# Attention with probabilities times values in plain float32, two groups of four heads in one PSUM tile

## The chip, the core and the metric

The kernel runs on one core of a Trainium2 chip. The metric is the device time of one execution in microseconds (us), as the median of several runs. The profile comes from one further execution, recorded instruction by instruction.

## The reference

A decoder trunk with two layers: sliding-window attention, then gated DeltaNet. 2048 tokens of width 1024 follow 16 meta tokens. Only the attention layer matters here (16 heads of 64, two heads of keys and values, so 8 query heads to each):

```python
s_band = einsum('bnqhgd,bnkhd->bnhgqk', qb, k_band) * scale      # blocks of 128 queries, 256 keys
s_meta = einsum('bnqhgd,bmhd->bnhgqm', qb, k_meta) * scale       # 16 meta tokens
s_band = where(valid_band, s_band - slopes * clipdist(dist_band), -inf)
s_meta = where(valid_meta, s_meta - slopes * clipdist(dist_meta), -inf)
p = softmax(concatenate([s_band, s_meta, sink], -1))
o = einsum(p_band, v_band) + einsum(p_meta, v_meta)
return (o * silu(gate)) @ w_out
```

Everything is float32 for the reference.

## The kernel before

The program is unrolled and built from tiles. A planner orders the instructions of each engine ahead of time from priorities (`high_priority(offset=...)` raises those of a block) and puts in all semaphores; at run time each engine takes its own list in order. A tile pool has a fixed number of buffers for each tag, and a new tile waits until the oldest is released.

Products that need float32 accuracy are mostly made in a reduced format (`F32R`, called fp32r in the profile): an operand is split into a high part, the cast, and a low part, the rest, and two or three products are added in PSUM. `mm3` (L60 to L63) makes three, `split` (L55 to L57) the two parts. A product of two plain `F32` tiles needs no split.

The stages: `attn_proj` (input projection; q, k, v and the gate go to DRAM; the gate comes last, transposed, with its store in L232), `attention`, then the DeltaNet stages `dn_proj` and `dn_scan`, which the change does not touch apart from comments. `attn_consts` runs between the q, k, v columns and the gate and makes masks and what belongs to the meta tokens.

`attention` goes over 17 tiles of tokens: 16 meta tokens, then 16 blocks of 128. A tile has four calls of `scores` and four of `values`, each for a group `hg` of 4 heads; `values` of a group comes four groups behind its `scores` (LAG, L493).

- `prep` (L335 to L377) loads q, k and v of the next tile and transposes them on TensorE; v is split into high and low halves of `vt` (L359, L360). The gate tile (L374) has one buffer.
- `scores` (L379 to L418), for each head: two products of the queries with 272 keys into `s_ps` (two buffers), then one VectorE operation that adds the distances and keeps the maximum (L395). For the 4 heads together: `nb`, `es` (L399 to L402), four exponentials on ScalarE (L405), the sum and its reciprocal (L408, L409). The meta probabilities are scaled (L411) and split into `px` on GpSimd (L413, L414); the band's are scaled on GpSimd (L416).
- `values` (L420 to L463), for 4 heads: the meta probabilities are transposed (L426) and copied into `mt` in four copies of 32 partitions, two on VectorE, two on ScalarE (L431, L433), so that each head's rows stand in its own columns only. Each of the two blocks of 128 keys is transposed, 4 heads into one PSUM tile (L440, pools `pt0` and `pt1`, one buffer each), then split: ScalarE casts `ph`, VectorE subtracts into `pl` (L443, L444). Five products of 512 columns go into `pv` (L447 to L449; one buffer): the stationary operand is 64 high and 64 low columns of v, so the upper 64 partitions of `pv` hold the part that comes from low v. ScalarE copies that part to `ob` (L451), VectorE adds it in two operations, one for each parity of heads, into `ot` (L453). GpSimd multiplies by the gate (L461), ScalarE and GpSimd split into `oh` and `ol` (L462, L463).
- `finish` (L465 to L478) is the output projection of a tile, 48 products of 512 columns by `mm3` into `ps_o`, cut into pieces that go between the other work.

Of the kernel before, what the change touches and what calls it, by code (L numbers as in the profile page):

```python
# [15 lines left out]
P = 128  # L16
# [22 lines left out]
def rsqrt(nc, pool, y, x, shape, tag):  # L39
    """y = x ** -0.5 for positive normal x."""  # L40
# [37 lines left out]
def norm_rows(nc, small, scr, xt, n, eng=None):  # L78
    """xt[:n] = rms_norm(xt[:n]) without its weight, which goes into the rows of the projection"""
# [15 lines left out]
def transpose_split(nc, psum, ident, xt, n, hi, lo, c0):  # L95
    """hi/lo[:, kt, c0:c0+n] = split(xt[:n].T)"""
# [10 lines left out]
def attn_proj(tc, a, sc, ident, hook):  # L107
    """q (normalised, ALiBi-scaled), k (normalised, twice), v and silu(gate)^T to DRAM."""
# [4 lines left out]
    with (  # L113
# [48 lines left out]
        def qkv_tile(cols, m, r0):  # L162
            """cols: (number of the column block, its weights)"""
# [52 lines left out]
        for c0 in (5, 7):  # L216
# [7 lines left out]
            for e, ct, (t0, n, hi, lo) in order:  # L224
# [7 lines left out]
                nc.sync.dma_start(sc["gate"][(c0 - 5 + e) * 2 + ct, :, t0:t0 + n], st[:, :n])  # L232


def attn_consts(tc, a, sc, ident, kp, tpp):
    """Masks with the distances, sinks, and what the meta tokens are as keys and values."""
# [43 lines left out]
    # v of the meta tokens, 8 times: for the high and the low parts of the probabilities of 4 heads  # L280
    vm = kp.tile([P, P], F32, name="vm")
    vmeta = kp.tile([P, 2, P], F32R, name="vmeta")
    for j in range(8):
        nc.sync.dma_start(vm[j * 16:j * 16 + 16, :], sc["kv"][0:NMETA, 256:384])
    vs = vm.rearrange("p (k d) -> p k d", k=2)
    split(nc, vmeta[:, :, 0:64], vmeta[:, :, 64:128], vs)
    return dict(tabs=tabs, sink=sink, sinkp=sinkp, nslope=nslope, wkk=wkk, kmeta=kmeta, vmeta=vmeta)


def attention(tc, a, sc, ident, ac):  # L290
    nc = tc.nc
    v = nc.vector
    with (
        tc.tile_pool(name="p2q", reuse_waits="tile", bufs=2) as lq,
        tc.tile_pool(name="p2s", reuse_waits="tile", bufs=4) as sp,
        tc.tile_pool(name="p2k", reuse_waits="tile", bufs=2) as lk,
        tc.tile_pool(name="p2p", reuse_waits="tile", bufs=5) as lx,
# [7 lines left out]
        tc.tile_pool(name="p2pt", reuse_waits="tile", bufs=2, space=PSUM) as tpp,  # L305
# [6 lines left out]
        tabs, sink, sinkp, nslope, wkk, kmeta, vmeta = (  # L312
# [985 lines left out]
```

## Time and profile before

| | |
|---|---|
| median of 3 runs | 3212.55 us (3207.07 to 3213.83) |
| span of the profiled execution | 3218.0 us |
| TensorE matmuls busy | 2994.2 us, 93% |
| VectorE busy | 2240.6 us, 70% |
| ScalarE busy | 1488.4 us, 46% |
| GpSimd busy | 969.5 us, 30% |
| TensorE clock granted, mean | 0.975 |

In the profile PE is TensorE's matmuls, PEld its weight loads, DVE VectorE, ACT ScalarE, POOL GpSimd, SP the engine that issues most DMAs. A row names the source line, the engine, the operation, the tile written and the tiles read. Matmuls overlap with one another, and a row's length has the way through the array in it, so the step from start to start tells what a product takes away from the next one, and its length doesn't. Shares of busy time are means over stages with different limits, so the stage of the change is read by itself.

### The profile page before, as it was taken

What the parts mean: (1) busy time and instruction counts of PE and PEld (TensorE: products, weight loads), DVE (VectorE), ACT (ScalarE), POOL (GpSimd) and SP (SyncE); (2) the same over time, 40 slices, a digit from 0 to 9 for tenths busy, and PEclk for the clock granted to TensorE, in tenths of its full rate; (3) what the DMA queues carried; (4) which work ended last, traced back from release to release, by engine and by line L of the source; (5) the groups of instructions that cost most, each with busy time, mean ns of one, the idle gap of its engine ahead of it and who ended that gap; (6) DMA issues with size and microseconds to landing.
All of it is one profiled execution on the core that took longest, in us unless ns stands there. A gap on an engine that the chain in (4) does not pass through costs nothing.

```text
span 3218.0 us, 54338 instructions
## 1 busy us (share of the span) xinstructions
PE 2994.2 (93%) x18685; PEld 2643.1 (82%) x18685; DVE 2240.6 (70%) x6092; ACT 1488.4 (46%) x4247; POOL 969.5 (30%) x1118
## 2 busy tenths in 40 slices
PE   6999998988888999999999989899989999999899
PEld 6999996776666999888999989898976777777687
DVE  6786028999897767897825767988148777788632
ACT  5513147776665453443325344332245665566421
POOL 3011004555453332321112222222144444444100
PEclk9999999999999999999999999999998999999899
DMA  4323122222223345346442434456455666565442
GB/s 116 98 70 100 60 81 91 80 77 67 71 75 101 102 114 128 101 123 167 145 115 78 121 102 111 104 145 192 129 158 146 171 184 182 170 173 159 153 139 98
DMA packets 553595, 385.92 MB, mean 120 GB/s; under 512 B 245512, under 2 KB 505352, under 8 KB 546152
## 3 DMA queue, kind: packets, MB, share of 16 engines
q1 hardware_dynamic: 517032, 365.05, 40.0%
q10 hardware_dynamic: 35952, 16.80, 1.9%
q0 software_dynamic: 336, 0.60, 0.3%
q8 instruction: 148, 2.42, 0.3%
q14 instruction: 127, 1.04, 0.1%
HBM read 245.38 MB, written 136.97 MB: 119 GB/s over the span
## 4 chain that ended last, share of the span: by engine, by line
PE 53%; DVE 27%; DMA 7%; ACT 6%; issue 5%; POOL 2%; SPq 1%; DVEq 0%; ACTq 0%; POOLq 0%
PE ps_d L61 5%; PE ps_d L62 5%; PE ps_d L63 5%; PE ps_o L61 4%; PE ps_o L62 4%; PE ps_o L63 4%; DVE acc L768 4%; PE r_ps L1110 3%; PE ds_ps L1137 3%; PE ps_mm L63 2%; PE ps_mm L61 2%; PE ps_mm L62 2%; DVE Xt L910 2%; PE o_ps L1141 2%; PE vn_ps L1126 2%
## 5 line engine op out<-in xcount | busy, mean ns | idle before, releaser
L61 PE MATMUL ps_d<-y_hi,wi_hi 128*128 128x384 f32 (+2 forms) x2304 | 752.4, 327 | 45.0 <-ACT u L762 38.5
L63 PE MATMUL ps_d<-y_hi,wi_lo 128*128 128x384 f32 (+2 forms) x2304 | 744.8, 323 | 0.0
L62 PE MATMUL ps_d<-y_lo,wi_hi 128*128 128x384 f32 (+2 forms) x2304 | 744.3, 323 | 0.0
L61 PEld LDWEIGHTS ps_d<-y_hi,wi_hi 128*128 128x128 f32 x2304 | 441.3, 192 | 59.0 <-ACT u L762 44.1
L63 PEld LDWEIGHTS ps_d<-y_hi,wi_lo 128*128 128x128 f32 x2304 | 441.8, 192 | 3.7 <-issue 3.4
L62 PEld LDWEIGHTS ps_d<-y_lo,wi_hi 128*128 128x128 f32 x2304 | 441.9, 192 | 1.9 <-issue 1.8
L640 POOL TENSOR_TENSOR wi_raw<-wi_raw,nw 128x1024 f32<-128x1024 f32 x96 | 207.2, 2159 | 642.0 <-DMA wi_raw<-in_dn_w_in 603.2
L57 DVE TENSOR_TENSOR wi_lo<-wi_raw,wi_hi 128x1024 fp32r<-128x1024 f32 x96 | 125.9, 1311 | 273.7 <-ACT wi_hi L56 270.8
L768 DVE SCALAR_TENSOR_TENSOR acc<-u,cw,acc 128x1040 f32<-128x1040 f32 (+1 forms) x192 | 284.4, 1481 | 6.4
L1112 POOL TENSOR_TENSOR S<-S,eL 128x256 f32<-128x256 f32 x248 | 157.6, 644 | 197.0 <-PE r_ps L1110 130.9
L61 PE MATMUL ps_o<-wo,oh 128*128 128x512 f32 x512 | 209.4, 409 | 3.7 <-ACT oh L56 2.9
L63 PE MATMUL ps_o<-wo,ol 128*128 128x512 f32 x512 | 204.7, 400 | 0.0
L1119 ACT ACTIVATE qs<-r_ps,ea 64x128 f32<-64x128 f32 x512 | 182.4, 362 | 47.1 <-DVE xp L1117 37.3
L62 PE MATMUL ps_o<-wo,oh 128*128 128x512 f32 x512 | 203.4, 397 | 0.0
L63 PE MATMUL ps_mm<-w_hi,y_lo 128*128 128x256 f32 (+1 forms) x680 | 193.2, 287 | 5.1 <-DVE y_lo L104 5.1
L61 PE MATMUL ps_mm<-w_hi,y_hi 128*128 128x256 f32 (+1 forms) x680 | 193.6, 287 | 4.0 <-DVE st L190 3.1
L1117 DVE SCALAR_TENSOR_TENSOR xp<-r_ps,c,bv_t 64x128 f32<-64x128 f32 x512 | 174.6, 343 | 30.3 <-ACT qs L1119 11.4
L62 PE MATMUL ps_mm<-w_lo,y_hi 128*128 128x256 f32 (+1 forms) x680 | 193.4, 286 | 0.0
L56 ACT CAST wi_hi<-wi_raw 128x1024 fp32r<-128x1024 f32 x96 | 100.5, 1046 | 160.2 <-PE ps_d L62 133.4
L1110 PE MATMUL r_ps<-S,kq_t 128*128 128x256 f32 x512 | 163.4, 407 | 4.3 <-ACT qs L1119 3.8
L405 ACT ACTIVATE p<-p,nb 128x272 f32<-128x272 f32 (+2 forms) x272 | 134.0, 495 | 51.2 <-DVE nb L400 50.7
L762 ACT COPY u<-ps_d 128x384 f32<-128x384 f32 (+2 forms) x192 | 84.1, 439 | 157.9 <-PE ps_d L63 157.8
(311 smaller groups left out, 7168.2 us busy)
## 6 DMA issues: line engine op xcount, KB each, us to landing
wi_raw<-in_dn_w_in SPq DMA_DIRECT2D x96, 512.0 KB, 4.3
kq_t<-d_kq SPq DMA_DIRECT2D x33, 512.0 KB, 5.8
bv_t<-d_bv SPq DMA_DIRECT2D x33, 512.0 KB, 5.2
x_t<-in_x SPq DMA_DIRECT2D x32, 512.0 KB, 3.6
d_kq<-kq SPq DMA_DIRECT2D x16, 1024.0 KB, 5.2
d_bv<-bv SPq DMA_DIRECT2D x32, 512.0 KB, 5.2
kt_t<-d_ktok SPq DMA_DIRECT2D x64, 256.0 KB, 4.3
z_t<-d_z SPq DMA_DIRECT2D x16, 1024.0 KB, 6.8
```

Of the source, the lines that this page charges most:

```text
L56: nc.scalar.copy(hi, src)
L57: nc.vector.tensor_tensor(lo, src, hi.bitcast(F32), op=ALU.subtract)
L61: nc.tensor.matmul(ps, lhsT=lh, rhs=rh, start=start, stop=False)
L62: nc.tensor.matmul(ps, lhsT=lh, rhs=rl, start=False, stop=False)
L63: nc.tensor.matmul(ps, lhsT=ll, rhs=rh, start=False, stop=stop)
L405: nc.scalar.activation(p4[:n, hh, k0:272], p4[:n, hh, k0:272], AF.Exp, bias=nb[:n, hh:hh + 1], scale=SLOPES[hg * 4 + hh], accum_out=z[:n, ...
L640: nc.gpsimd.tensor_tensor(raw, raw, nw.unsqueeze(2).to_broadcast([P, KT, P]), op=ALU.mult)
L768: v.scalar_tensor_tensor(acc[:, :ncol], in0=u[:, j:j + ncol], scalar=cw[:, ct, j:j + 1], in1=acc[:, :ncol], op0=ALU.mult, op1=ALU.add)
L1110: nc.tensor.matmul(r, lhsT=kq[:, g, :], rhs=S[:, g], start=True, stop=True)
L1112: nc.gpsimd.tensor_tensor(S[:, g], S[:, g], pers["eL"][hf][:, :, g, n].unsqueeze(2).to_broadcast([P, 2, P]), op=ALU.mult)
L1117: v.scalar_tensor_tensor(xp[hb[h]], in0=r[0:64, h, :], scalar=pers["c1"][hf][hb[h], g, n:n + 1], in1=bv[hb[h], g, :], op0=ALU.mult, op1=AL ...
L1119: nc.scalar.activation(qs[hb[h]], r[64:128, h, :], AF.Copy, scale=pers["ea"][hf][hb[h], g, n:n + 1])
```

## The change

Eight heads, all that share one head of keys and values, are handled in one call, and the calls become generators that the outer loop takes forward in five steps for each group, with pieces of `prep` and `finish` between them.

- The product of probabilities and values is made in plain float32: v goes in straight from the loaded tile `kv` as 64 stationary columns, the transposed probabilities as plain float32 `ph` (copied, three of four times by ScalarE, once by VectorE). `pl`, `vt`, `px`, `ob` and the additions into `ot` are gone.
- Heads 0 to 3 of a group (e = 0) go to partitions 0 to 63 of `pv`, heads 4 to 7 (e = 1) to 64 to 127.
- The meta probabilities are transposed unsplit, 8 heads by 16 rows; one VectorE operation makes `mt` by a product with a mask `mrow`.
- VectorE multiplies `pv` by the gate as it reads it. The order of heads in `ot` differs, so the gate is stored in another order (two DMAs in place of one) and the rows of the output weights are loaded in another order (two DMAs in place of one).
- The gate tile has two buffers, `kv` four, `ph` six; the two pools of transposed probabilities become one with two buffers; `p8` has three buffers of 8 heads where `p4` had five of 4.

Comments that the diff takes away elsewhere are left out here.

```diff
...
-                nc.sync.dma_start(sc["gate"][(c0 - 5 + e) * 2 + ct, :, t0:t0 + n], st[:, :n])
+                for x in range(2):
+                    hd = ((c0 - 5 + e) * 2 + ct) * 2 + x
+                    r = hd % 8 // 4 * 64
+                    nc.sync.dma_start(sc["gate"][hd // 8 * 4 + hd % 4, r:r + 64, t0:t0 + n],
+                                      st[x * 64:x * 64 + 64, :n])
...
-    vm = kp.tile([P, P], F32, name="vm")
-    vmeta = kp.tile([P, 2, P], F32R, name="vmeta")
+
+    vmeta = kp.tile([P, 2, 2, 64], F32, name="vmeta")
+    nc.gpsimd.memset(vmeta, 0.0)
     for j in range(8):
-        nc.sync.dma_start(vm[j * 16:j * 16 + 16, :], sc["kv"][0:NMETA, 256:384])
-    vs = vm.rearrange("p (k d) -> p k d", k=2)
-    split(nc, vmeta[:, :, 0:64], vmeta[:, :, 64:128], vs)
-    return dict(tabs=tabs, sink=sink, sinkp=sinkp, nslope=nslope, wkk=wkk, kmeta=kmeta, vmeta=vmeta)
+        nc.sync.dma_start(vmeta[j * 16:j * 16 + 16, j // 4],
+                          sc["kv"][0:NMETA, 256:384].rearrange("m (k d) -> m k d", k=2))
+
+    mrow = kp.tile([P, 4], F32, name="mrow")
...
+    return dict(tabs=tabs, sink=sink, sinkp=sinkp, nslope=nslope, wkk=wkk, kmeta=kmeta, vmeta=vmeta, mrow=mrow)
...
-        tc.tile_pool(name="p2s", reuse_waits="tile", bufs=4) as sp,
+        tc.tile_pool(name="p2s", reuse_waits="tile", bufs=3) as sp,
         tc.tile_pool(name="p2k", reuse_waits="tile", bufs=2) as lk,
-        tc.tile_pool(name="p2p", reuse_waits="tile", bufs=5) as lx,
+        tc.tile_pool(name="p2p", reuse_waits="tile", bufs=3) as lx,
...
-        tc.tile_pool(name="p2p0", reuse_waits="tile", bufs=1, space=PSUM) as pt0,
-        tc.tile_pool(name="p2p1", reuse_waits="tile", bufs=1, space=PSUM) as pt1,
+        tc.tile_pool(name="p2p0", reuse_waits="tile", bufs=2, space=PSUM) as ptp,
...
+            w = a["attn_w_out"][0].rearrange("(v e h d) c -> v h e d c", v=2, e=2, h=4)
             for k in range(KT):
                 for c in range(2):
                     raw = lk.tile([P, 512], F32, tag="wraw", name="wo_raw")
                     cs = slice(c * 512, c * 512 + 512)
-                    nc.sync.dma_start(raw, a["attn_w_out"][0][k * P:(k + 1) * P, cs])
+                    for e in range(2):
+                        nc.sync.dma_start(raw[e * 64:e * 64 + 64], w[k // 4, k % 4, e, :, cs])
                     split(nc, who[k][:, cs], wlo[k][:, cs], raw)
...
-                kv = lq.tile([P, 384], F32, tag="kv", name="kv_t")
+                kv = lq.tile([P, 384], F32, tag="kv", bufs=4, name="kv_t")
...
-                vt = wk.tile([P, 2, P], F32R, tag="vt", name="vt")
-                vsrc = kv[:, 256:384].rearrange("p (k d) -> p k d", k=2)
-                nc.scalar.copy(vt[:, :, 0:64], vsrc)
-                nc.gpsimd.tensor_tensor(vt[:, :, 64:128], vsrc, vt[:, :, 0:64].bitcast(F32), op=ALU.subtract)
...
-            gt = lp.tile([P, KT, P], F32, tag="gate", bufs=1, name="gate_t")
+            gt = lp.tile([P, KT, P], F32, tag="gate", bufs=2, name="gate_t")
...
+        def scores(t, kvh):
...
+                if hh in (1, 3, 5):
+                    yield
...
-            pm = lx.tile([P, 4, 16], F32, tag="pm", bufs=5, name="pm")
-            v.tensor_tensor(pm[:n], p4[:n, :, 256:272], z[:n].unsqueeze(2).to_broadcast([n, 4, 16]), op=ALU.mult)
-            px = lx.tile([P, 4, 2, 16], F32R, tag="px", bufs=5, name="px")
-            nc.gpsimd.tensor_copy(px[:n, :, 0], pm[:n])
-            nc.gpsimd.tensor_tensor(px[:n, :, 1], pm[:n], px[:n, :, 0].bitcast(F32), op=ALU.subtract)
+            pm = lx.tile([P, 8, 16], F32, tag="pm", name="pm")
+            v.tensor_tensor(pm[:n], p8[:n, :, 256:272], z[:n].unsqueeze(2).to_broadcast([n, 8, 16]), op=ALU.mult)
             if i is not None:
-                nc.gpsimd.tensor_tensor(p4[:n, :, k0:256], p4[:n, :, k0:256],
-                                        z[:n].unsqueeze(2).to_broadcast([n, 4, 256 - k0]), op=ALU.mult)
-            c["p", hg] = (p4, px)
-
-        def values(t, hg):
-            """Attention output of 4 heads, transposed."""
+                for e in range(2):
+                    es_ = slice(e * 4, e * 4 + 4)
+                    nc.gpsimd.tensor_tensor(p8[:n, es_, k0:256], p8[:n, es_, k0:256],
+                                            z[:n, es_].unsqueeze(2).to_broadcast([n, 4, 256 - k0]), op=ALU.mult)
+            c["p", kvh] = (p8, pm)
+            yield
...
+
             c = ctx[t]
-            n, i, kvh, ot = c["n"], c["i"], hg // 2, wk.tile([P, 2, P], F32, tag="ot", name="ot")
-            p4, px = c.pop(("p", hg))
+            n, i = c["n"], c["i"]
+            p8, pm = c.pop(("p", kvh))
+            blocks = [] if i is None else [(128, c["kv"])] if i == 0 else [(0, ctx[t - 1]["kv"]), (128, c["kv"])]
             tm = tpp.tile([P, P], F32, tag="tp", bufs=2, name="tm")
-            nc.tensor.transpose(tm[:, :n], px[:n].rearrange("p h e m -> p (h e m)").bitcast(F32), ident[:n, :n])
...
+            nc.tensor.transpose(tm[:, :n], pm[:n].rearrange("p h m -> p (h m)"), ident[:n, :n])
+            mt = wk.tile([P, 4, P], F32, tag="mt", bufs=2, name="mt")
+            v.tensor_tensor(mt[:, :, :n], tm[:, :n].unsqueeze(1).to_broadcast([P, 4, n]),
+                            mrow.unsqueeze(2).to_broadcast([P, 4, n]), op=ALU.mult)
+            terms = []
+            for b0, kv in blocks:
+                for e in range(2):
+                    pt = ptp.tile([P, 4, P], F32, tag="pt", name="pt")
+                    for hh in range(4):
+                        nc.tensor.transpose(pt[:, hh, :n], p8[:n, e * 4 + hh, b0:b0 + 128], ident[:n, :n])
+                    ph = wk.tile([P, 4, P], F32, tag="ph", bufs=6, name="ph")
+                    if e and b0:
+                        v.tensor_copy(ph[:, :, :n], pt[:, :, :n])
+                    else:
+                        nc.scalar.copy(ph[:, :, :n], pt[:, :, :n])
+                    terms.append((e, kv[:, 256 + kvh * 64:256 + kvh * 64 + 64], ph))
+                    yield
+            terms += [(e, vmeta[:, e, kvh, :], mt) for e in range(2)]
             pv = vpp.tile([P, 4, P], F32, tag="pv", name="pv")
...
+            for j, (e, vt, ph) in enumerate(terms):
+                nc.tensor.matmul(pv[e * 64:e * 64 + 64, :, :n], lhsT=vt, rhs=ph[:, :, :n], start=j < 2,
+                                 stop=j >= len(terms) - 2)
+            if kvh == 0:
                 c["xt"] = xp.tile([P, D], F32, tag="x", name="x_t")
                 nc.sync.dma_start(c["xt"][:n], x_rows(a, i))
                 c["oh"] = lp.tile([P, KT, P], F32R, tag="oh", name="oh")
                 c["ol"] = lp.tile([P, KT, P], F32R, tag="ol", name="ol")
-            ks = slice(hg * 2, hg * 2 + 2)
+            ks = slice(kvh * 4, kvh * 4 + 4)
             oh, ol = c["oh"][:, ks, :n], c["ol"][:, ks, :n]
-            nc.gpsimd.tensor_tensor(ot[:, :, :n], ot[:, :, :n], c["gt"][:, ks, :n], op=ALU.mult)
+            ot = wk.tile([P, 4, P], F32, tag="ot", bufs=2, name="ot")
+            v.tensor_tensor(ot[:, :, :n], pv[:, :, :n], c["gt"][:, ks, :n], op=ALU.mult)
             nc.scalar.copy(oh, ot[:, :, :n])
             nc.gpsimd.tensor_tensor(ol, ot[:, :, :n], oh.bitcast(F32), op=ALU.subtract)
+            yield
 
...
-        slots = [(t, hg) for t in range(len(tiles)) for hg in range(4)]
+        slots = [(t, kvh) for t in range(len(tiles)) for kvh in range(2)]
 
         fin = None
         pre = None
-        LAG = 4
+        LAG = 2
         for j in range(len(slots) + LAG):
-            with tc.high_priority(offset=150 + (1000 if j < 12 else 0)):
-                if j < len(slots):
-                    t, hg = slots[j]
-                    if hg == 0:
+            boost = 1000 if j < 6 else 0
+            sg = vg = None
+            if j < len(slots):
+                t, kvh = slots[j]
+                with tc.high_priority(offset=150 + boost):
+                    if kvh == 0:
                         for _ in pre or ():
                             pass
                         pre = prep(t + 1) if t + 1 < len(tiles) else None
-                    scores(t, hg)
-                    next(pre, None) if pre else None
-                    next(pre, None) if pre and hg == 0 else None
-            with tc.high_priority(offset=250 + (1000 if j < 12 else 0)):
-                if j >= LAG:
-                    t, hg = slots[j - LAG]
-                    if hg == 3:
-                        for _ in fin or ():
-                            pass
-                    values(t, hg)
-                    if hg == 3:
-                        fin = finish(t)
-            for _ in range(2):
-                next(fin, None) if fin else None
+                sg = scores(t, kvh)
+            if j >= LAG:
+                t, kvh = slots[j - LAG]
+                if kvh == 1:
+                    for _ in fin or ():
+                        pass
+                vg = values(t, kvh)
+            for step in range(5):
+                with tc.high_priority(offset=150 + boost):
+                    next(sg, None) if sg else None
+                    if step in (1, 2, 4) and pre:
+                        next(pre, None)
+                with tc.high_priority(offset=250 + boost):
+                    next(vg, None) if vg else None
+                if step < 4 or not vg:
+                    next(fin, None) if fin else None
+            if j >= LAG and slots[j - LAG][1] == 1:
+                fin = finish(slots[j - LAG][0])
...
```

## Rows read from the trace of the kernel before

**Rows 1.** Page, part 2: busy tenths of two engines in 40 slices

```profile
PE   6999998988888999999999989899989999999899
...
DVE  6786028999897767897825767988148777788632
```

**Rows 2.** Stretches: length, then each engine's busy us and instructions, clock, DMA

```profile
300.00:475.00 175.00, 174.32 (x982) 166.63 (x981) 25.12 (x104) 50.37 (x123) 13.95 (x24) 1.00 0.25 80
475.00:1010.00 535.00, 467.53 (x2427) 368.46 (x2425) 473.01 (x1480) 369.15 (x1120) 267.49 (x376) 0.97 0.25 80
...
560.00:990.00 430.00, 378.02 (x1981) 301.46 (x1980) 383.16 (x1160) 291.37 (x886) 222.76 (x307) 0.98 0.23 74
```

**Rows 3.** Who TensorE's products waited for, 560 to 990 us: total, times, longest

```profile
PE pv L447 <- DVE ot L453: 18.1, 21, 3.0
PE pt L440 <- DVE pl L444: 10.8, 20, 1.5
PE s_ps L393 <- DVE mx L395: 9.0, 19, 1.0
PE tm L426 <- DVE mt L431: 6.4, 5, 2.2
```

**Rows 4.** VectorE by line, 475 to 1010 us: busy us, mean ns, idle

```profile
L444 DVE TENSOR_TENSOR pl<-pt,ph 128x512 fp32r<-128x512 f32 x124 | 84.3, 684 | 10.1 <-ACT ph L443 9.2
L453 DVE TENSOR_TENSOR ot<-pv,ob 64x256 f32<-64x256 f32 x128 | 53.0, 414 | 3.8 <-ACT ob L451 2.2
...
L431 DVE CAST mt<-tm 32x128 fp32r<-32x128 f32 x128 | 37.1, 290 | 6.7 <-ACT mt L433 2.7
L399 DVE TENSOR_TENSOR nb<-mx,sinkp 128x4 f32<-128x4 f32 x64 | 24.6, 384 | 0.9
...
L400 DVE TENSOR_TENSOR nb<-nb,nslope 128x4 f32<-128x4 f32 x64 | 21.4, 334 | 1.0
```

**Rows 5.** ScalarE by line, same stretch

```profile
L443 ACT CAST ph<-pt 128x512 fp32r<-128x512 f32 x124 | 70.7, 584 | 26.4 <-PE pv L447 25.3
...
L451 ACT COPY ob<-pv 64x512 f32<-64x512 f32 x64 | 37.3, 583 | 3.3 <-PE pv L449 1.9
...
L433 ACT CAST mt<-tm 32x128 fp32r<-32x128 f32 x128 | 32.5, 254 | 41.9 <-DVE mt L431 32.2 <-PE tm L426 8.0
```

**Rows 6.** GpSimd by line, same stretch

```profile
L461 POOL TENSOR_TENSOR ot<-ot,gate_t 128x256 f32<-128x256 f32 x64 | 47.4, 741 | 88.3 <-DVE ot L453 85.3 <-DMA gate_t<-d_gate 3.0
...
L414 POOL TENSOR_TENSOR px<-pm,px 128x64 fp32r<-128x64 f32 x64 | 20.6, 322 | 2.2
L413 POOL CAST px<-pm 128x64 fp32r<-128x64 f32 x64 | 16.0, 250 | 11.5 <-DVE pm L411 4.6 <-PE pv L449 2.3 <-DVE nb L399 2.3
```

**Rows 7.** Timeline: start and length in us, engine, line, operation, idle before

```profile
704.33 0.84 DVE L453 TENSOR_TENSOR ot<-pv,ob 64x256 f32<-64x256 f32 x2
...
705.33 0.47 PE L447 MATMUL pv<-ph,vt 128*128 128x512 f32 x1 [0.59 <-DVE ot L453]
...
705.63 0.39 PE L448 MATMUL pv<-pl,vt 128*128 128x512 f32 x1
...
706.32 0.39 PE L449 MATMUL pv<-mt,vmeta 128*128 128x512 f32 x1
```

**Rows 8.** Timeline of TensorE in the scan of the DeltaNet stage

```profile
2599.80 0.38 PE L1110 MATMUL r_ps<-S,kq_t 128*128 128x256 f32 x1
...
2601.08 0.61 PE L1110 MATMUL r_ps<-S,kq_t 128*128 128x256 f32 x2
```

**Rows 9.** Timeline of TensorE in the DeltaNet projection

```profile
1201.77 1.04 PE L813 MATMUL tp_k<-ident,kq 128*128 128x128 f32 x8
1202.74 1.09 PE L848 MATMUL g_ps<-kq 128*64 128x128 f32 x16
1203.76 0.45 PE L61 MATMUL ps_d<-y_hi,wi_hi 128*128 128x400 f32 x1
```

**Rows 10.** The products into g_ps: ns shortest, median, longest; first and last start

```profile
L848 PE MATMUL g_ps<-kq x528: 272/273/444, 1087.7 to 2179.7; 128*64 128x128 f32 x176
```

More of the change, by code (lines that the diff above doesn't have):

```diff
@@ L304, in attention @@
         tc.tile_pool(name="p2x", reuse_waits="tile", bufs=2) as xp,
[L305 removed]
+        tc.tile_pool(name="p2pt", reuse_waits="tile", bufs=1, space=PSUM) as tpp,
         tc.tile_pool(name="p2ps", reuse_waits="tile", bufs=2, space=PSUM) as spp,
         tc.tile_pool(name="p2pv", reuse_waits="tile", bufs=1, space=PSUM) as vpp,
[L308 to L309 removed]
+        tc.tile_pool(name="p2p0", reuse_waits="tile", bufs=2, space=PSUM) as ptp,
         tc.tile_pool(name="p2pp", reuse_waits="tile", bufs=1, space=PSUM) as pp,
     ):
[L312 to L317 removed]
+        tabs, sink, sinkp, nslope, wkk, kmeta, vmeta, mrow = (
+            ac[n] for n in ("tabs", "sink", "sinkp", "nslope", "wkk", "kmeta", "vmeta", "mrow"))
         who, wlo = [], []
@@ L343, in prep @@
             if i is None:
-                kwin = vt = None
+                kwin = None
             else:
@@ L427, in values @@
-            mt = mts[hg % 2]
-            for hh in range(4):
-                ps = slice(hh * 32, hh * 32 + 32)
-                if hh % 2:
-                    v.tensor_copy(mt[ps, hh, :n], tm[ps, :n])
-                else:
-                    nc.scalar.copy(mt[ps, hh, :n], tm[ps, :n])
-            blocks = [] if i is None else [(128, c["vt"])] if i == 0 else [(0, ctx[t - 1]["vt"]), (128, c["vt"])]
-            pv = vpp.tile([P, 4, P], F32, tag="pv", name="pv")
-            pts = []
-            for (b0, vt), ptp in zip(blocks, (pt0, pt1)):
-                pt = ptp.tile([P, 4, P], F32, tag="pt", name="pt")
-                for hh in range(4):
-                    nc.tensor.transpose(pt[:, hh, :n], p4[:n, hh, b0:b0 + 128], ident[:n, :n])
-                ph = wk.tile([P, 4, P], F32R, tag="ph", name="ph")
-                pl = wk.tile([P, 4, P], F32R, tag="pl", name="pl")
-                nc.scalar.copy(ph[:, :, :n], pt[:, :, :n])
-                v.tensor_tensor(pl[:, :, :n], pt[:, :, :n], ph[:, :, :n].bitcast(F32), op=ALU.subtract)
-                pts.append((vt, ph, pl))
@@ L446, in values @@
-            for bi, (vt, ph, pl) in enumerate(pts):
-                nc.tensor.matmul(pv[:, :, :n], lhsT=vt[:, kvh, :], rhs=ph[:, :, :n], start=bi == 0, stop=False)
-                nc.tensor.matmul(pv[:, :, :n], lhsT=vt[:, kvh, :], rhs=pl[:, :, :n], start=False, stop=False)
-            nc.tensor.matmul(pv[:, :, :n], lhsT=vmeta[:, kvh, :], rhs=mt[:, :, :n], start=not blocks, stop=True)
-            ob = wk.tile([64, 4, P], F32, tag="ob", bufs=2, name="ob")
-            nc.scalar.copy(ob[:, :, :n], pv[64:128, :, :n])
@@ L478, in finish @@
             yield
-        def run(gen, k=1):
-            for _ in range(k):
-                if gen is None or next(gen, 0) == 0:
-                    return
         with tc.high_priority(offset=200):
```

49 lines of the change are left out of this document (27 added, 22 removed).

## The prediction, made before the changed kernel ran

> **What bounds the kernel now.** I read the shares of the span in slices first, to find the stage that the change touches. The attention is the stretch of 80 us slices in which VectorE stands at 8 or 9 tenths and TensorE at 8 to 9 [rows 1]; before it VectorE is nearly idle and TensorE full. Then the table by stretches: from 475 to 1010 us, the 535 us in which attention runs, TensorE is busy 467.5 us, VectorE 473.0, ScalarE 369.2, GpSimd 267.5 [rows 2]. No engine is full. TensorE idles 535 - 467.5 = 67.5 us, and of these 430 - 378.0 = 52.0 lie in the even middle from 560 to 990 us. In the projection ahead, from 300 to 475 us, TensorE is busy 174.3 of 175 us [rows 2]. So these 67.5 us are what this stage could give back at most, as long as TensorE's own work doesn't grow.
>
> Third, who makes TensorE wait in that middle. All the long waits are on VectorE: 18.1 us of pv for the additions into ot, 10.8 of the transposes for pl, 9.0 of the scores for the maximum, 6.4 of the transposed meta probabilities for the copies into mt [rows 3]. The timeline shows one such wait: the two additions run from 704.33 to 705.17, TensorE stands 0.59 us, then the five products of 512 columns follow, the second at 705.63 and the fifth at 706.32, so 0.23 us apart [rows 7]. So VectorE, at 88 to 89% and in order, holds up an in-order TensorE. The question is whether the change takes more from that chain than it puts on TensorE.
>
> **The change part by part, for 8 heads (two calls of values before, one after); 32 of them, two with one block of keys in place of two, and two small ones for the 16 meta tokens, which I leave out.**
>
> VectorE loses pl (124 x 0.684 = 84 us), the two additions into ot (128 x 0.414 = 53), half of the mt copies (128 x 0.290 = 37) [rows 4]. It gains, for each 8 heads, three operations on 128 x 512 from PSUM: the product that makes mt, the product with the gate and one copy ph. I price them as pl, which reads the same shape from PSUM, at 0.684: 3 x 0.684 x 32 = 66. The copy has no row of its own; its bounds are ScalarE's 0.584 for the same shape [rows 5] and pl's 0.684, no matter here. The small operations on 4 columns become half as many on 8; the two steps of nb alone are 24.6 + 21.4 us, so half of them is -23 [rows 4]. VectorE: 473 - 84 - 53 - 37 + 66 - 23 = 342 us of 535.
>
> ScalarE loses ob (37.3), its half of mt (32.5) and a quarter of the ph copies (70.7 / 4 = 18) [rows 5]: 369 - 88 = 281. GpSimd loses the gate (47.4) and the split of px (20.6 + 16.0) [rows 6]: 267 - 84 = 183. None of the three can bound the stage any more. TensorE is the only engine left near it.
>
> TensorE. Before, 8 heads take 10 products of 512 columns at 0.23 us from start to start [rows 7]: 2.30 us. After, they take 6 products in plain float32. How long is one? The state product r_ps is plain float32 of 256 columns. It stands as two records, 0.61 us together where one alone is 0.38, so the second starts 0.23 us behind the first [rows 8]; that is twice the time for a column of the reduced format, and twice over. For 512 columns that makes 2 x 2 x 0.23 = 0.92 us. g_ps gives it finer and shows something else: eight plain float32 products of 64 stationary columns, which go by turns to the lower and the upper 64 partitions of one tile, are 16 records of 128 columns in 1.09 us; the 8 transposes ahead of them, of 128 columns too and one behind the other, take 1.04 [rows 9]. So two records go side by side: less the 0.27 us of the last one [rows 10], seven steps take 0.82 us, 0.12 each with a longer first one, and the transposes' 0.77 / 7 = 0.11. I take 0.11 us for each pair. The new pv products are made the same way (64 stationary columns, e = 0 to the lower, e = 1 to the upper partitions, in turns). At 512 columns a pair of records is 4 x 0.11 = 0.44 us, a pair of products 0.88, three pairs 2.64: +0.34 us on the 2.30. One transpose of px less is -0.11. Going into and out of the half-width form costs 0.2 us in place of 0.11, read from the last transpose to the first g_ps and from the last g_ps to ps_d [rows 9]: +0.2 for both. Sum +0.43 us for 8 heads, 32 times: +14 us.
>
> The trace has no pair in which the second product has to wait for a copy of its own. In the change each ph comes from its own copy, and between the products the planner may put transposes or scores, which break a pair. Per 8 heads the cost of this lies between 0 and three lone products, 3 x 0.88 = 2.64 us. I take one lone product more in every fourth group, 0.88 x 8 = +7 us, near the lower end: the five old pv products stand back to back in the timeline, though four of them hang on copies of their own [rows 7].
>
> The idle time. The waits for ot, pl and the mt copies are 18.1 + 10.8 + 6.4 = 35.3 of the 52 us [rows 3]. The operations behind them go: pv is now released by one operation in place of the copy ob and two additions, half as often; pt is released by one copy in place of copy and subtraction; mt by one operation in place of eight copies. In proportion, over the whole stage, 35.3 x 67.5 / 52 = 46 us. I let the wait for the maximum and the rest stand, since the 16 maxima of a tile stay as they are. What is late next is TensorE itself.
>
> A new wait: the gate product waits on VectorE for the last pv product, and behind it queue the maxima of the next heads, for which the scores wait with two buffers. Before, the additions into ot stood in the same place. So I add nothing, with 0.68 us x 32 = 22 us as the upper bound and zero below.
>
> Hidden edits: the gate's store is two DMAs in place of one (five column chunks by eight blocks, 40 to 80), on SP's queue in the stretch in which TensorE is full [rows 2]; kv_t, q_t and the output weights queue behind them, so without that cover it would be a late start of attention, at most some us. The loads of the output weights double in number and keep their bytes. The zeroing of vmeta, mrow and its transpose come once, in the same stretch. The second gate buffer can only help. I keep 5 us each way for the start and the end of the stage.
>
> Sum: -46 + 14 + 7 = -25 us. The profiled execution spans 3218.0 us, 0.2% over the median of 3212.55; the stage's difference is taken off the median: 3187.5, so 3187 us.
>
> One rule of the Trainium skill speaks against the change. FP8 and Floating Point Precision, TensorE Precision Notes, says that true FP32 takes four passes through the array; the trace agrees for one product alone, 0.92 us against 0.23. By that rule without the side-by-side halves, the sum is that of the first rival.
>
> **The rivals.**
> First, the pairs don't form, and it gets slower. Mechanism: a product of e = 0 is queued as soon as its ph is there, transposes or scores stand between it and its partner, and each runs alone. All six alone are 5.28 us in place of 2.64, +2.64 x 32 = +84, and with -46 + 14 the kernel comes to +52: 3265. Two lone products more in each group would give -32 + 56 = +24: 3236. It decides from 32 / 32 = 1 us, a little over one lone product for 8 heads. For it: old pv had to wait for its buffer, which let its copies pile up; new pv doesn't have to. Against it: g_ps, and e alternates, so that a shifted pair is still a pair.
> Second, the waits move: with two groups in flight in place of four, a chain of 8 maxima, 8 exponentials and two products on GpSimd has less slack, and TensorE waits for the probabilities or for ScalarE's copies. If 21 of the 46 us stay lost, the sum is near zero: 3212. For it: the chain of 8 heads is twice as long and one buffer less is free. Against it: ScalarE and GpSimd fall to about 281 and 183 of 535 us.
> Third, TensorE closes nearly all gaps: -67 + 14 = -53: 3159.
>
> **How the numbers follow.** Forecast 0.58, first rival 0.20, second 0.12, third 0.10. The likeliest one's own range is 3170 to 3205 (the bounds of the new wait and of the ends). The range for 8 in 10 takes in most of the third and the milder half of the first rival: 3157 to 3238. A difference of 0.2%, 6.4 us, is about what can be told from none. Faster is the forecast's 0.57 and the third's 0.10, a little of the others: 0.68. Same is most of the second: 0.12. Slower is the first: 0.20.
>
> **What would show it.** In the changed profile: the stage's VectorE near 340 us, ScalarE near 280, GpSimd near 185; pv records of 128 x 512 with 64 columns that start within some ns of each other, two by two, and a fresh pair each 0.44 us; no wait of TensorE for an operation behind pv that costs over a few us in total. Wrong it is if pv records start alone, one each 0.43 us with other products between them; if TensorE's idle time in the stage stays near 67 us under new names (ph, p, z); or if the stage's gain is there and the DeltaNet stages behind it, which no line of the change touches, give it back.

## The result, and the profile of the changed kernel

The changed kernel takes **3230.31 us** as the median of 20 runs (3213.39 to 3240.85), the kernel before 3213.19 us (3200.37 to 3221.29, 20 runs beside it): ratio **1.0055, interval [1.0042, 1.0067]**. It is 17 us slower, where 25 us faster had been forecast. The profiled execution of the changed kernel spans 3214.7 us, at the low end of its runs. The two profiled executions differ by 9 us ahead of the change already (the last product of the q, k, v columns starts at 300.0 us before, at 291.0 after), and by another 9 us behind it, in the DeltaNet stages that no line of the change touches (2212.7 us before, 2203.9 after). So the stage is compared by itself and not by the spans.

First the stretches of the changed kernel, columns as in [rows 2]: length, busy us and instructions of TensorE, its weight loads, VectorE, ScalarE and GpSimd, clock, DMA.

```profile
475.00:1010.00 535.00, 515.01 (x2395) 326.05 (x2394) 316.31 (x967) 258.84 (x787) 170.94 (x129) 0.97 0.25 78
560.00:990.00 430.00, 420.15 (x1972) 267.54 (x1973) 250.74 (x742) 200.94 (x617) 143.96 (x101) 0.99 0.23 70
```

In these 535 us VectorE falls from 473.0 to 316.3 us, ScalarE from 369.2 to 258.8, GpSimd from 267.5 to 170.9. TensorE's idle time falls from 67.5 to 20.0 us, and in the even middle from 52.0 to 9.9 us. All this is what the change was to do. But the stage has become longer. From the last product of the gate to the last product of attention's output it takes 517.3 us before (488.0 to 1005.3) and 532.4 after (478.4 to 1010.8): +15.1 us, near the 17 us between the medians.

Who TensorE waited for in the changed kernel, 560 to 990 us (total, times, longest), against [rows 3]:

```profile
PE tm L441 <- DVE pm L425: 5.0, 5, 1.3
PE s_ps L405 <- DVE mx L407: 4.2, 14, 0.5
PE ps_o L61 <- DVE x_t L487: 0.3, 1, 0.3
PE qps L377 <- DVE mt L443: 0.2, 1, 0.2
```

The waits for ot, pl and mt (35.3 us) are gone, and no wait for ph, p or z has taken their place. TensorE is now itself what is late. In the chain of waits over the whole span its share goes from 53% to 64%, VectorE's from 27% to 21%; these lines begin part 4 of the page, before and after:

```profile
PE 53%; DVE 27%; DMA 7%; ACT 6%; issue 5%; POOL 2%; SPq 1%; DVEq 0%; ACTq 0%; POOLq 0%
```

```profile
PE 64%; DVE 21%; DMA 5%; ACT 4%; issue 3%; POOL 1%; SPq 1%; DVEq 0%; ACTq 0%; POOLq 0%
```

What TensorE does with the time is seen in the table of stretches for the products into pv alone (length, busy us and records, clock, DMA): before, then after.

```profile
475.00:1010.00 535.00, 96.69 (x314) 0.97 0.25 80
```

```profile
475.00:1010.00 535.00, 153.09 (x380) 0.97 0.25 78
```

The pv products take 56 us more. The records give the balance of the whole stage, when the time from each start to the next is put down to the product that started first (idle time falls to the product ahead of it):

| from the last gate product to the last output product, us | before | after | |
|---|---|---|---|
| pv | 88.4 | 147.5 | +59.1 |
| scores | 121.2 | 104.2 | -17.0 |
| transposes | 93.5 | 77.6 | -15.9 |
| output projection | 214.2 | 203.2 | -11.0 |
| stage | 517.3 | 532.4 | +15.1 |

So three kinds of work give back 44 us, and pv takes 59. The timeline of TensorE in the changed kernel shows how (start and length in us, line, operation, tile, shape, count):

```profile
705.39 0.39 PE L63 MATMUL ps_o<-wo_hi,ol 128*128 128x512 f32 x1
705.71 1.07 PE L461 MATMUL pv<-ph,kv_t 128*64 128x512 f32 x2
706.72 0.66 PE L450 MATMUL pt<-ident,p 128*128 128x128 f32 x4
707.13 0.37 PE L405 MATMUL s_ps<-kwin,qst 128*128 128x272 f32 x1
707.34 0.29 PE L406 MATMUL s_ps<-kwin,qst 128*128 128x272 f32 x1
707.46 0.27 PE L450 MATMUL pt<-ident,p 128*128 128x128 f32 x1
707.66 1.07 PE L461 MATMUL pv<-ph,kv_t 128*64 128x512 f32 x2
708.66 0.55 PE L450 MATMUL pt<-ident,p 128*128 128x128 f32 x3
...
709.40 1.07 PE L461 MATMUL pv<-ph,kv_t 128*64 128x512 f32 x2
710.40 0.39 PE L405 MATMUL s_ps<-kwin,qst 128*128 128x272 f32 x1
710.63 0.29 PE L406 MATMUL s_ps<-kwin,qst 128*128 128x272 f32 x1
710.85 0.64 PE L461 MATMUL pv<-ph,kv_t 128*64 128x512 f32 x1
710.86 0.64 PE L461 MATMUL pv<-mt,vmeta 128*64 128x512 f32 x1
```

Each product is two records. At 705.71, 707.66 and 709.40 a product stands alone between other work, and the next work starts 1.00 us later (706.72, 708.66, 710.40). Only the fourth has a partner: at 710.85 and 710.86 two records start 6 ns apart, one for each half of the array (heads 0 to 3 write the lower 64 partitions of `pv`, heads 4 to 7 the upper). In the list of TensorE the 192 products (six for 8 heads; fewer in the first block and for the meta tokens) stand in 117 runs, a run being products with no other work between them: 78 products alone, 7 runs of two, 28 of three, 4 of four. So the first rival came true: in 22 of the 30 groups with six products the first three stand alone, with transposes and scores between each and its partner. In five groups a shifted pair did form, of the second and the third.

### The profile page after: what moved, and what is told of

The parts are those of the page before. It is cut to its first block, busy times and chain, and to the rows that moved or that the text cites. A ratio compares the mean times of both kernels' runs of the same rounds, so it can differ in the third digit from the quotient of the medians.

```text
span 3214.7 us, 53174 instructions
## 1 busy us (share of the span) xinstructions
PE 3044.7 (95%) x18720; PEld 2602.8 (81%) x18720; DVE 2083.8 (65%) x5593; ACT 1379.7 (43%) x3922; POOL 871.4 (27%) x866
## 4 chain that ended last, share of the span: by engine, by line
PE 64%; DVE 21%; DMA 5%; ACT 4%; issue 3%; POOL 1%; SPq 1%; DVEq 0%; ACTq 0%; POOLq 0%
PE ps_o L61 5%; PE ps_o L63 5%; PE ps_o L62 5%; PE ps_d L61 5%; PE ps_d L62 5%; PE ps_d L63 5%; PE pv L461 4%; DVE acc L780 4%; PE r_ps L1122 3%; PE ds_ps L1149 3%; PE ps_mm L61 2%; PE ps_mm L63 2%; PE ps_mm L62 2%; PE vn_ps L1138 2%; PE o_ps L1153 2%
## 5 line engine op out<-in xcount | busy, mean ns | idle before, releaser
L61 PE MATMUL ps_d<-y_hi,wi_hi 128*128 128x384 f32 (+2 forms) x2304 | 752.7, 327 | 45.1 <-ACT u L774 37.3
L63 PEld LDWEIGHTS ps_d<-y_hi,wi_lo 128*128 128x128 f32 x2304 | 441.8, 192 | 3.7 <-issue 3.6
L407 DVE CUSTOM_DVE_ANT_0 p<-s_ps,tab 128x272 f32<-128x272 f32 (+2 forms) x272 | 106.5, 411 | 91.0 <-PE s_ps L406 89.2
L429 POOL TENSOR_TENSOR p<-p,z 128x1024 f32<-128x1024 f32 (+1 forms) x64 | 118.6, 1872 | 160.0 <-DVE z L423 100.8
```

The lines of the kernel that those rows point to most:

```text
L61: nc.tensor.matmul(ps, lhsT=lh, rhs=rh, start=start, stop=False)
L63: nc.tensor.matmul(ps, lhsT=ll, rhs=rh, start=False, stop=stop)
L429: nc.gpsimd.tensor_tensor(p8[:n, es_, k0:256], p8[:n, es_, k0:256], z[:n, es_].unsqueeze(2).to_broadcast([n, 4, 256 - k0]), op=ALU.mult)
```

## The experiments

Two theories were set against each other. **A:** the change does give back the 46 us that VectorE cost, and the broken pairs in pv take them and more. **B:** the waits move or the new frame (8 heads in one call, five steps to a group) costs the time, and the form of the products matters little. (In the first four expectations theory 1 is a part of A, and theory 2 is worded anew in each.) The median of before beside the first four kernels is 3211.35 us (11 runs), beside the last four 3213.81 us (17 runs).

### Partners side by side, two or four products in a run

```diff
+            terms = [terms[j ^ 1] for j in range(len(terms))]
-            for j, (e, vt, ph) in enumerate(terms):
-                nc.tensor.matmul(...)
+            with tc.high_priority(offset=600):
+                for j, (e, vt, ph) in enumerate(terms):
+                    nc.tensor.matmul(...)
```

Of the two products of a block, the one whose probabilities come last (e = 1) now goes first, so that its partner is ready when it is queued. The work is the same.

> Only the order of the pv products on TensorE changes against the changed kernel: within a block of keys the product of heads 4 to 7, whose copy is ready last, is put ahead of that of heads 0 to 3, and both get a higher priority. In the order of TensorE's list 192 products then stand in 32 runs of two and 32 of four, where the changed kernel has 78 alone, 7 runs of two, 28 of three and 4 of four. Theory 1 (lone half-width products are what made it slower): from the changed kernel's trace a lone product takes 1.00 us from its start to the next foreign one and each further pair adds 0.86, so 32 x (1.00 + 1.86) = 92 us in place of 147, that is 40 to 60 us less: 3170 to 3190 us, which is faster than the kernel before (3213). Theory 2 (TensorE isn't what sets the end, or two halves don't go side by side at 512 columns): less than 10 us change, 3220 to 3232.

Measured: 3167.25 us, ratio 0.9863 [0.9842, 0.9884], a little under the range of theory 1. The list has 32 runs of two and 32 of four, and no product alone. The stretch for pv alone:

```profile
475.00:1010.00 535.00, 95.52 (x380) 0.97 0.28 86
```

The same work, in another order, takes 95.5 us in place of 153.1, and the kernel some 62 us less than the change as it was given. The frame is the same in both, so theory B falls. Two things were changed at once here, order and priority; the last two experiments take them apart.

### All six products in one run, in pairs

```diff
+            terms = terms[2:4][::-1] + terms[0:2] + terms[4:]
+            with tc.high_priority(offset=600):
+                with tc.issue_after(last.ins):
                     for j, (e, vt, ph) in enumerate(terms):
...
```

The order is second block, first block, meta, in pairs of different halves: from product to product e is 1, 0, 0, 1, 0, 1. (The expectation says that neighbours are always in different halves; the second and the third are not.) None may be queued ahead of the last transpose (`last`).

> All six pv products of a group in one run, queued behind the last transpose of the group, neighbours always in different halves. Theory 1: 1.00 + 2 x 0.86 = 2.72 us for a group, 87 us in all against 147 in the changed kernel: 3165 to 3190. If instead the wait for the last copy then shows as a gap ahead of the run, some 0.5 us for a group or 16 us in all are lost against the kernel with runs of two and four. Theory 2: within 10 us of the changed kernel, 3220 to 3232.

Measured: **3160.2 us**, ratio 0.9835 [0.9814, 0.9857], the fastest version of the whole computation here; it beats both kernels, and lies 5 us under the range expected. Its timeline, then its stretch for pv alone:

```profile
707.88 1.94 PE L463 MATMUL pv<-ph,kv_t 128*64 128x512 f32 x8
709.65 1.03 PE L463 MATMUL pv<-mt,vmeta 128*64 128x512 f32 x4
710.61 0.39 PE L405 MATMUL s_ps<-kwin,qst 128*128 128x272 f32 x1
```

```profile
475.00:1010.00 535.00, 88.08 (x380) 0.96 0.28 86
```

Six products run from 707.88 to the next start at 710.61: 2.73 us, three steps at 0.86 and 0.14 for the way in and out. A step is a pair side by side, or a product without a partner. The prediction had 2.64 and 0.2.

### The same run of six, sorted by halves

```diff
+            terms = terms[1::2][::-1] + terms[0::2]
+            terms = [terms[k] for k in (1, 0, 2, 3, 4, 5)]
```

Three products of the upper half (second block, meta, first block), then three of the lower.

> As the run of six with neighbours in different halves, but first the three products of heads 4 to 7, then the three of heads 0 to 3, so only the third and the fourth can go side by side. Instructions, copies, waits and the place of the run are otherwise alike. Theory 1: five steps of 0.86 in place of three, 4.4 us for a group against 2.72, so some 50 us more than the paired run: about 3225. Theory 2 (pairing has no price, only the number of breaks has): the same as the paired run.

Measured: 3177.02 us, ratio 0.9897 [0.9879, 0.9914]: 17 us over the paired run, not 50. The direction is theory A's, the size is a third. The stretch for pv alone and one run in the timeline:

```profile
475.00:1010.00 535.00, 117.01 (x380) 0.97 0.27 85
```

```profile
595.26 1.07 PE L466 MATMUL pv<-ph,kv_t 128*64 128x512 f32 x2
596.17 0.59 PE L466 MATMUL pv<-mt,vmeta 128*64 128x512 f32 x1
596.18 0.64 PE L466 MATMUL pv<-ph,kv_t 128*64 128x512 f32 x1
596.60 0.59 PE L466 MATMUL pv<-mt,vmeta 128*64 128x512 f32 x1
596.66 1.45 PE L466 MATMUL pv<-ph,kv_t 128*64 128x512 f32 x5
597.95 1.02 PE L466 MATMUL pv<-mt,vmeta 128*64 128x512 f32 x2
598.90 0.40 PE L405 MATMUL s_ps<-kwin,qst 128*128 128x272 f32 x1
```

The run takes 3.64 us. Four steps of 0.86 and 0.14 for the way in and out make 3.58; I had counted five steps, 4.44. A product of ph starts at 596.18, 5 ns beside the second one (mt of the upper half, 596.17). The third of the list uses the upper half too, which is busy until 597.03; so this must be the fourth, for the idle lower half, ahead of its place. One by one, the twelve records fit two series of six: starts at 595.27, 595.75, 596.18, 596.60, 597.03 and 597.46, and at 596.18, 596.66, 597.09, 597.52, 597.95 and 598.38. The records don't name the block, so this rests on the half being busy.

### The kernel before, with VectorE relieved of its largest pieces

```diff
-                pl = wk.tile([P, 4, P], F32R, tag="pl", name="pl")
-                v.tensor_tensor(pl[:, :, :n], pt[:, :, :n], ph[:, :, :n].bitcast(F32), op=ALU.subtract)
-                pts.append((vt, ph, pl))
+                pts.append((vt, ph, ph))
...
-            ob = wk.tile([64, 4, P], F32, tag="ob", bufs=2, name="ob")
-            nc.scalar.copy(ob[:, :, :n], pv[64:128, :, :n])
-            for e in range(2):
-                v.tensor_tensor(ot[e * 64:e * 64 + 64, :, :n], pv[0:64, e::2, :n], ob[:, e::2, :n], op=ALU.add)
+            v.tensor_copy(ot[:, :, :n], pv[:, 0:2, :n])
```

The low part of the probabilities and the joining of the two halves of pv are left out (ph is used twice); all products stay.

> The kernel before with VectorE and ScalarE relieved alone: the subtraction into pl is left out (the second product takes ph again) and one VectorE copy of 128 x 256 takes the place of ob and the two additions into ot. TensorE's products are the same in number and form. The low parts of the probabilities and of the values are left out of the result. Theory 1's other half (the waits for pl and ot are idle time that comes back): (18.1 + 10.8) x 67.5 / 52 = 37 us less than the kernel before: about 3176. Rival (the waits move to the maxima, mt or the exponentials): less than 15 us gained, over 3198.

Measured: 3157.44 us, ratio 0.9831 [0.9812, 0.985]: -54 us, more than the 37 by the rows of the waits. So VectorE's work did hold up the kernel before, and by more than the waits named after pl and ot show. ScalarE's copy into ob (37.3 us, [rows 5]) went with it, so the 54 us are not VectorE's alone; the next experiment takes away an operation of VectorE only.

### The subtraction into pl alone

Only the first part of the edit above; ph is counted twice in place of ph and pl.

> The kernel before without the subtraction into pl: ph stands for both products, so the low part of the probabilities is left out of the sum; all of TensorE's work stays. VectorE loses 124 x 0.684 = 84 us in the stage. Theory by the table of waits: the wait for pl, 10.8 us in the middle, 14 in the whole stage, is what goes: about 3199. Rival by load (VectorE is in order, so an operation less lets all that stands behind it come earlier, and the waits on ot, on the maximum and on mt shrink too): 30 to 45 us, so 3168 to 3183.

Measured: 3181.5 us, ratio 0.9903 [0.989, 0.9916]: -32 us. The row of the wait for pl would have given 14 us, and the rival by load comes out. Who TensorE waited for in this kernel, 560 to 900 us, and the stage:

```profile
PE s_ps L393 <- DVE mx L395: 6.8, 13, 1.7
PE pv L445 <- DVE ot L451: 6.7, 11, 2.2
...
PE tm L426 <- DVE mt L431: 0.7, 3, 0.3
```

```profile
475.00:1010.00 535.00, 479.04 (x2552) 388.22 (x2551) 429.26 (x1430) 375.10 (x1131) 273.26 (x384) 0.96 0.27 84
```

Before, the same 340 us showed:

```profile
PE pv L447 <- DVE ot L453: 14.3, 18, 3.0
PE pt L440 <- DVE pl L444: 7.9, 16, 1.5
PE s_ps L393 <- DVE mx L395: 7.0, 15, 1.0
PE tm L426 <- DVE mt L431: 5.5, 4, 2.2
```

The waits for ot fall from 14.3 to 6.7 us, those for mt from 5.5 to 0.7, and those for pl are gone. The wait for the maximum, which the rival had shrink too, hardly moved (7.0 before, 6.8 here), and that for x_t rose from 1.0 to 5.8. So with one operation less in VectorE's list, others behind it come earlier too. A table of waits shows who was late, not who made him late.

### The frame without the plain float32 products

The changed kernel with the old products put back: px, four copies into mt, ph and pl, five products for 4 heads, ob and one addition, the gate on GpSimd. What is left of the change is the call for 8 heads, the order of gate and output weights, the halved small operations, the joined pools of transposed probabilities and the steps.

```diff
-                    terms.append((e, kv[:, 256 + kvh * 64:256 + kvh * 64 + 64], ph))
+                    v.tensor_tensor(pl[:, :, :n], pt[:, :, :n], ph[:, :, :n].bitcast(F32), op=ALU.subtract)
+                    pts.append((vt, ph, pl))
...
-            for j, (e, vt, ph) in enumerate(terms):
-                nc.tensor.matmul(pv[e * 64:e * 64 + 64, :, :n], lhsT=vt, rhs=ph[:, :, :n], ...)
+                for bi, (vt, ph, pl) in enumerate(pts):
+                    nc.tensor.matmul(pv[:, :, :n], lhsT=vt[:, kvh, :], rhs=ph[:, :, :n], ...)
+                    nc.tensor.matmul(pv[:, :, :n], lhsT=vt[:, kvh, :], rhs=pl[:, :, :n], ...)
```

> The frame of the change alone: 8 heads in one call, generators, the new order of gate and output weights, halved small operations, but the products of the kernel before (high and low half of v, ph and pl, four copies into mt, five products of 512 columns for 4 heads, ob and an addition). Theory A: the kernel before loses its time to VectorE, and the change gives it back by taking pl, the additions and the mt copies away. VectorE then still holds pl (84 us) and the mt copies (37) here, loses about half of the small operations (23) and half of the additions' fixed cost, and stands near 430 of 535 us; TensorE idles 45 to 60 us in the stage, and the kernel takes 3195 to 3210 us against 3213 before. Theory B: the frame (other priorities, five steps to a group) is what closes the gaps. Then TensorE idles near 20 us as in the changed kernel, pv takes about 88 us, and the kernel takes 3160 to 3175 us.

Measured: 3197.35 us, ratio 0.9952 [0.9941, 0.9964]. So the frame by itself doesn't make the kernel slower: it gives 15 us. The stage:

```profile
475.00:1010.00 535.00, 470.99 (x2399) 375.11 (x2399) 441.80 (x1246) 356.31 (x1044) 252.16 (x248) 0.92 0.27 85
```

VectorE stands at 441.8 us here, and TensorE still idles 535 - 471.0 = 64.0 us, against 67.5 before and 20.0 in the changed kernel. That is over the 45 to 60 us of theory A and far from the 20 of theory B: the frame is not what closes the gaps. Of TensorE's list of 316 products, 38 stand alone in this frame too, and it hardly matters for them: a lone old product takes 0.31 us to the next other start, a run of five 1.26, so 0.25 each. Where in the span the 15 us lie the two profiles don't settle: this one's stage is as long as before's (516.3 against 517.3 us), with the clock at 0.92 in it against 0.97.

### Order without priority, and priority without order

```diff
+            terms = [terms[j ^ 1] for j in range(len(terms))]
```

> The changed kernel with the order of the two products of a block turned round (heads 4 to 7 first, the product whose probabilities come last), with no other priority. TensorE's list then holds 30 products alone, 17 runs of two and 32 of four. Theory A: 0.86 us x 111 steps + 0.14 x 79 runs = 106 us of pv in the stage, 13 more than the version with pairs and 41 less than the changed kernel: 3175 to 3190. Rival (priority decides): 3220 to 3235.

Measured: 3179.5 us, ratio 0.9893 [0.9874, 0.9912].

```profile
475.00:1010.00 535.00, 110.67 (x380) 0.96 0.28 87
```

```diff
+            with tc.high_priority(offset=600):
                 for j, (e, vt, ph) in enumerate(terms):      # order as in the change
```

> The changed kernel with its products raised by 600 in priority, in their old order within a block. In TensorE's list this leaves 78 products alone, 5 runs of two, 24 of three and 8 of four, nearly as in the changed kernel (78, 7, 28, 4). Theory A (how often a run of products is broken is what costs): 0.86 us for each of about 147 steps and 0.14 for each of 115 runs, 143 us for pv in the stage, so the changed kernel's time within some us: 3222 to 3235. Rival (the products come too late in TensorE's list, and their priority is what the version with pairs gained by): near 3167.

Measured: 3227.62 us, ratio 1.0039 [1.0026, 1.0053].

```profile
475.00:1010.00 535.00, 151.14 (x380) 0.99 0.25 80
```

Priority alone leaves the runs nearly as they were, and the time too. Turning each pair round, one line, brings -34 us against before and about -51 against the change; with the priority on top, which is the version with pairs, another 12 us go. From starts, pv takes 107.3 us in the stage with the order alone (106 expected) and 145.3 with the priority alone (143). Put together:

| | runs in TensorE's list, by length | pv busy in the stage, us | median, us | ratio to before |
|---|---|---|---|---|
| changed kernel | 78 of 1, 7 of 2, 28 of 3, 4 of 4 | 153.1 | 3230.3 | 1.0055 |
| priority alone | 78 of 1, 5 of 2, 24 of 3, 8 of 4 | 151.1 | 3227.6 | 1.0039 |
| sorted by halves | 30 of 6, not in pairs | 117.0 | 3177.0 | 0.9897 |
| order alone | 30 of 1, 17 of 2, 32 of 4 | 110.7 | 3179.5 | 0.9893 |
| pairs | 32 of 2, 32 of 4 | 95.5 | 3167.3 | 0.9863 |
| six in pairs | 30 of 6, 2 of 4, 2 of 2 | 88.1 | 3160.2 | 0.9835 |

From the last row to the first pv grows by 65.0 us and the time by 70. The one that falls off the line is the kernel sorted by halves: 29 us more pv than the paired run, 17 us more time. Measured as above, from the last product of the gate to the last of attention's output, the stage takes 532.4, 523.4, 488.5, 476.2, 470.0 and 465.8 us in the order of the table, against 517.3 before; there the kernel sorted by halves is 22.7 us over the paired run. Each of these is one execution.

## Why the prediction was wrong

**Idle time: right.** The term was -46 us; in the same 535 us TensorE idles 47.5 us less. The number is partly luck. Its working went by the rows of the waits, and the kernel without pl shows that these understate one operation (14 for 32 us); taking "in proportion, over the whole stage" made up for it here.

**Engines: right, a little too high.** Predicted 342, 281 and 183 us, measured 316, 259 and 171. The three operations on 128 x 512 that the change adds cost 22.1, 22.0 and 21.9 us, just the 66 of the sum:

```profile
L471 DVE TENSOR_TENSOR ot<-pv,gate_t 128x512 f32<-128x512 f32 x32 | 22.1, 691 | 43.8 <-PE pv L461 37.6 <-issue 6.1
L453 DVE COPY ph<-pt 128x512 f32<-128x512 f32 x32 | 22.0, 688 | 46.1 <-PE pt L450 46.0
L443 DVE TENSOR_TENSOR mt<-tm,mrow 128x512 f32<-128x512 f32 x32 | 21.9, 686 | 8.0 <-PE tm L441 7.8
...
L414 DVE TENSOR_TENSOR nb<-nb,nslope 128x8 f32<-128x8 f32 x32 | 14.6, 455 | 0.7
...
L413 DVE TENSOR_TENSOR nb<-mx,sinkp 128x8 f32<-128x8 f32 x32 | 7.4, 232 | 0.4
```

The rest of the gap is in the small operations: the two steps of nb fell from 24.6 + 21.4 [rows 4] to 7.4 + 14.6, and I had priced only these, at -23; es, z and its reciprocal were halved too, from 50.2 us together to 22.6.

**The new wait: right.** No wait of TensorE for the gate product stands in its table; the gate product itself now waits 37.6 us for pv (above), on an engine that has time.

**A pair: right, a pair's surroundings too dear.** 0.88 us forecast, 0.86 measured; three pairs with the way in and out 2.73 against 2.84. But the +14 us counted before at five products back to back, 2.30 for 8 heads. From starts the pv of before takes 88.4 us, 2.76 for 8 heads, since some of its products stand apart and wait for copies; with all six in pairs the new pv takes 87.9. So that term was about 0, not +14. (Of the two figures 4.0 and 1.9 us are idle time by the profile; without it they are 84.4 and 86.0.)

**How often a pair is broken: the step that failed.** I took "one lone product more in every fourth group", +7 us, near the lower end of 0 to 2.64 us for 8 heads, because the old products stand back to back. The list has 149 steps in place of the 96 of the paired run and 117 runs in place of 34. At 0.86 us for a step and 0.14 for a run (fitted to the medians of lone products, 1.00 us, and of full runs, 2.73) that is 45.6 + 11.6 = 57 us over the paired run, of the 59.6 measured (147.5 against 87.9). For a group of 8 heads that is 1.8 us, beyond the 1 us from which the first rival was said to decide. Of the rival's two cases, "two lone products" (56 us, 3236) is nearly what came; "six alone" (3265) lies far above. That 3230 lies within the stated 3157 to 3238 is owed to the part of the range that was left to this rival, not to the forecast's sum.

The fault was the analogy, and it was read from one group. The trace of before does show that its list breaks groups: of the 60 groups of 4 heads with five products, 33 stand as five in a row, 26 as four and, later, the product of mt alone, one as three and two. One of the 26, in the timeline before:

```profile
714.54 0.27 PE L426 MATMUL tm<-ident,px 128*128 128x128 f32 x1
714.65 0.60 PE L440 MATMUL pt<-ident,p 128*128 128x128 f32 x4
715.00 0.49 PE L449 MATMUL pv<-mt,vmeta 128*128 128x512 f32 x1
715.33 0.60 PE L366 MATMUL qps<-ident,q_t 128*128 128x128 f32 x4
```

For the old form a break costs 0.06 us a product (0.31 against 0.25), so it hardly shows in the time; for the new form a broken pair costs a whole step. And the argument "a shifted pair is still a pair" held in five groups of 30 only: mostly each of the first three products stands alone, since its partner needs a copy that comes later and other work stands in the list between them.

The rule of the Trainium skill on true FP32 (FP8 and Floating Point Precision, TensorE Precision Notes) that I had set against the change holds for a product without a partner: a step of 0.86 us against 0.23 in the old form, 3.7 to 1. Had the pairs formed, the third rival would have been the nearest by its number: it gave 3159, the paired run of six took 3160. That would have been luck too: TensorE still idles 24.2 us in that kernel's stage, so not nearly all gaps close, and it is the +14 that isn't there.

## What to carry to other kernels

Where a form of product is only cheap beside a partner, order the list so that the partner is ready first (issue first the one whose data comes last), and look at the order of the engine's list, not only at the dependencies: one line was worth 51 us here. Taking an operation off an in-order engine that was busy 88% of the stage gave more than the row of its waits (32 us for 14). When a gain in idle time is right and the time still rises, look in the same stretch for an engine whose busy time has grown by more.

## What the runs showed that was not expected

- A product on the lower half of TensorE started beside one on the upper half although another product for the upper half stands between them in the list (596.18 us, above). The Trainium skill (TensorE: Matmul & The Clock Gate, Part 3) says of packed products that they start and end strictly in the order of the program; the run of six in 3.64 us, four steps and not five, speaks against it.
- A run of half-width products between full-width ones costs 0.14 us on top of its steps; with 117 runs in place of 34 that is 12 us. The Trainium skill (TensorEngine Tiling (Array Packing), Tiling Modes) says that a change of tiling mode drains the engine. The 0.14 us fit that but don't show it: a break costs the old full-width products 0.06 us as well.
- The first step of nb, which reads two tiles of 4 columns, takes 145 to 165 ns when GpSimd runs nothing beside it (19 of 64 in the stage before), and up to 1506 ns, median 424, when it overlaps an operation of GpSimd (45 of 64). All 33 that take longer than 165 ns end within 30 ns of the end of an operation of GpSimd. In the changed kernel 13 of 32 overlap one, and 5 of the 32 take over 400 ns. So part of VectorE's relief may come from the work taken from GpSimd; it wasn't tried by itself.
